# Quarter-wise first modulations in a two-layer hybrid diffusion block on one Trainium2 core

## The chip, the cores and the metric

The kernel runs on one core of one Trainium2 chip. The time is the device time of one execution in microseconds (us). Three runs of the kernel before are at hand, and one more execution was taken with the hardware profiler; every row below is from that one. Engines are named as in the profile: PE is TensorE's matmul and PEld its weight load, DVE is VectorE, ACT is ScalarE, POOL is GpSimd, SP is SyncE, which here issues the loads.

## What is computed

Two layers of a transformer-like trunk act on 512 tokens (256 latent, 256 context) of 1024 features. Each layer is a SwiGLU feed-forward half-step, three attention branches that are gated and merged, and a second feed-forward half-step. Each of these parts starts with a normalisation whose gain and shift come from a conditioning vector, the modulation:

```python
def adaln(h, g, shift, scale):
    return rms_norm(h, g) * (1 + scale) + shift

mx = jnp.split(cond_x @ ada_w[l] + ada_b[l], N_MOD, axis=-1)   # N_MOD = 9, each of 1024 features
x = x + 0.5 * mx[2] * swiglu(adaln(x, ffn1_norm[l], mx[0], mx[1]), ffn1_w_in[l], ffn1_w_out[l])
```

The context stream uses the same weights with its own conditioning vector. The change touches only the first two modulations of the first layer, `mx[0]` (shift) and `mx[1]` (scale), for both streams. They stand at the head of everything: no feed-forward product can be made before some of the normalised, modulated features are there.

## The kernel before

Activations are held transposed: features on the 128 partitions, tokens along the row. So the 1024 features are `KD` = 8 blocks `k` of 128, and a normalised activation is a pair of tiles `hh`, `hl` (a rounded part and the remainder) per block. Every weight is split in the same way into `whi` (by ACT) and `wlo` (by DVE), and one product of a 128-column weight block with a feature block is three matmuls (`mm3`, lines 101 to 103): `whi` with `hh`, `whi` with `hl`, `wlo` with `hh`, each 512 tokens wide.

`run()` opens the kernel by hand:

- `load_x` loads the eight blocks of x and sums their squares (lines 340 to 357).
- `ahead(4)` loads the first halves (feature blocks 0 to 3) of the four weight chunks that the first products use, two gate and two up chunks. Their second halves are loaded later (`second_half`, lines 166 to 168), released by a POOL copy that waits for a certain part of `ada_w`.
- `ada_first(c, slots)` works out half `c` of the two modulations. It loads eight slots of 128x1024 (feature block `k` of the conditioning vector by 512 columns of each modulation; line 288), then yields; then for each `k` it makes four matmuls of 256 columns, one on each group of 32 array columns (`ada_product`, line 280), and yields after each `k`. `set_mods` copies the sums from PSUM (DVE, line 302), yields, transposes them (PE, line 306), adds the bias (DVE, line 312) and makes the gain `G` (DVE, line 322).
- Half 0 (`first`) is worked out between the steps of the two norms. Line 1212 then multiplies x by the norm for both token halves on DVE (`vh` and `th` hold token half 0, `p` token half 1).
- `modulate(k)` makes `hh` and `hl` of block `k`, for each token half: ACT line 409 makes `hh`, POOL line 408 makes the unrounded value `w`, DVE line 410 subtracts.
- `products` makes the first 32 products (8 blocks `k`, 4 accumulators), in the order of `k`. Half 1 (`rest`) is worked out beside the first ten of them, by this list, and blocks 4 to 7 are modulated after it:

```python
at = [1, 2, 3, 4, 5, 6, 7, 8, 8, 10]
```

PE's order is the program's own. On the other engines and on the loads' queue a scheduler sets the order when the kernel is built, and each engine then works through its list in that order. The split weights live in rings of eight `whi` and eight `wlo` tiles; the eight halves of the first four chunks fill both, so the split of a later chunk needs a tile that PE has finished with.

Of the kernel before, what the change touches and what calls it, by code (L numbers as in the profile page):

```python
# [13 lines left out]
D = 1024  # L14
KD = 8
# [43 lines left out]
class Kernel:  # L59
# [221 lines left out]

    def ada_first(self, c, slots):

        acc = self.P("v", (128, 256))
        raws = []
        for k, raw in enumerate(slots):
            src = self.t["ada_w"][0, 0:2, k, :, c * 512:(c + 1) * 512]
            self.nc.sync.dma_start(out=raw.rearrange("p (m n) -> p m n", m=2), in_=src.rearrange("m p n -> p m n"))
        yield
        for k, raw in enumerate(slots):  # L290
            for g in range(4):
                self.ada_product(acc, g, self.cond[:, k], raw[:, g * 256:(g + 1) * 256], k == 0, k == KD - 1)
            yield
        yield from self.set_mods(acc, [(0, 0), (0, 1)], 4 * c, 2)

    def set_mods(self, acc, mods, k0, nj):

# [884 lines left out]
    def run(self):  # L1182
        nc = self.nc
        self.setup()
        self.done = set()
        self.load_x()
        slots = []
        for i in (6, 5, 4, 3, 1, 0):
            c = self.T(f"m{i}", [128, 2, 1024])
            slots += [c[:, j] for j in range(2)]  # L1190
        for tag in ("pth", "ptl"):
            slots += [self.T(tag, [128, 1024], bufs=2) for _ in range(2)]
        slots = slots[:KD], slots[KD:]
        self.new_h()

        self.first, self.late = True, []
        self.ahead(4)
        first = self.ada_first(0, slots[0])
        next(first)
        rest = self.ada_first(1, slots[1])  # L1200
        next(rest)
        late = [second_half(slots[1][4][0:1, 0:1]) for second_half in self.late]
        self.late = None
        norms = [self.norm(0, 0, half, False) for half in range(2)]
        xn = [self.T(tag, [128, NT], bufs=1 if tag == "th" else 3) for tag in ("vh", "vh", "vh", "th", "p", "p", "p")]
        xn = [v[:, h] for v in xn for h in HALF]
        xn = [xn[:KD], xn[KD:]]
        for half in (0, 1, 0, 1):
            next(first)
            R = next(norms[half])  # L1210
            for v, x in zip(xn[half] if R else (), self.x):
                nc.vector.tensor_tensor(out=v, in0=x[:, HALF[half]], in1=R, op=ALU.mult)
        for _ in first:
            pass

        def modulate(k):
            for half in range(2):
                self.modulate(0, 0, half, k, R, xn[half][k] if k < len(xn[half]) else None)

        def products(accs, rhs):  # L1220

            self.begin(slots[1][-1][0:1, 0:1])
            for take in late:
                take()

            at = [1, 2, 3, 4, 5, 6, 7, 8, 8, 10]
            for n in range(KD * len(accs)):
                k, (acc, wt) = n // len(accs), accs[n % len(accs)]
                self.col_product(wt, KD, rhs, acc, slice(0, NT), (k, k + 1))
                while at and at[0] == n + 1:  # L1230
                    at.pop(0)
                    next(rest)
                    if not at:
                        for kk in range(KD // 2, KD):
                            modulate(kk)
            self.setup2(slots[1][-1][0:1, 0:1])

        for k in range(KD // 2):
            modulate(k)
        self.first = products  # L1240

        pend = {
            (0, 0): [(0, m) for m in range(2, 8)],
            (0, 1): [(0, 8), (1, 0), (1, 1), (1, 2)],
            (1, 0): [(1, m) for m in range(3, 9)],
            (1, 1): [],
        }

        def ffn(l, f, halves, after):

            self.steps = self.ada(pend[l, f]) if pend[l, f] else iter(())
            gap = PACE[l, f]
            done = [0]

            def fill(blocks):
                done[0] += blocks
                while done[0] >= gap > 0:
                    done[0] -= gap
                    next(self.steps, None)

            self.ffn(l, f, halves, fill, after)
            for _ in self.steps:
                pass

        for l in range(DEPTH):
            last = l == DEPTH - 1

            def then_norm(ll, n):
                def after(half):
                    if half == 0:  # L1270
                        self.new_h()
                    ticks = [1, 3, 4, 5] if half == 0 else [3, 5, 5, 5] if n == 1 else [1, 2, 2, 2]
                    self.pending.append([0, self.norm(ll, n, half), ticks])
                return after

            ffn(l, 0, (0, 1), then_norm(l, 1))
            self.mixer(l, last, then_norm(l, 2))
            if last:
                ffn(l, 1, (0,), lambda half: None)
            else:  # L1280
                ffn(l, 1, (0, 1), then_norm(l + 1, 0))
        for k in range(KD):
            nc.sync.dma_start(out=self.out[k], in_=self.x[k][:, 0:256])
# [3 lines left out]
def _layout(inputs):  # L1287
    import numpy as np

    f = {k: np.asarray(v) for k, v in inputs.items()}  # L1290
    f32 = np.float32
    o = {}
    o["x"] = np.concatenate([f["x"][0], f["ctx"][0]], 0).T.reshape(KD, 128, NT)
    o["cond"] = np.stack([f["c"][0], f["c_ctx"]], -1).reshape(KD, 128, 2).transpose(1, 0, 2)
    o["ada_w"] = f["ada_w"][:1].reshape(1, KD, 128, 9, D).transpose(0, 3, 1, 2, 4)[:, :2]
    o["ada_t"] = f["ada_w"].reshape(DEPTH, D, 9, KD, 128).transpose(0, 2, 3, 4, 1)
    o["condb"] = np.repeat(np.stack([f["c"][0], f["c_ctx"]])[None], 128, axis=0)
    o["ada_b"] = f["ada_b"].reshape(DEPTH, 9, KD, 128).transpose(3, 0, 1, 2)
# [33 lines left out]
    for n in ("a_q_norm", "a_k_norm", "b_q_norm", "b_k_norm"):  # L1332
        g = f[n][:, p64]
        row += [g, np.roll(g, 32, axis=1)]
    for n in ("c_q_norm", "c_k_norm"):
        g = f[n][:, p96]
# [9 lines left out]
    q, k = np.arange(128)[:, None], np.arange(128)[None, :]  # L1346
    o["mask"] = np.concatenate([np.where(k <= q, 0, NEG), np.where(k >= q, 0, NEG)], 1).astype(f32)
    for n, dim in (("cs64", 64), ("cs32", 32)):
# [5 lines left out]
        c, s = np.cos(ang).astype(f32), np.sin(ang).astype(f32)  # L1354
# [27 lines left out]
```

## Time and profile before

| | us |
|---|---|
| median of 3 runs | 2152.4 (2151.74 to 2154.44) |
| profiled execution, its own time | 2153.58 |
| profiled execution, span of the records | 2151.8 |
| PE busy in the span | 2097.2 (97%) |
| DVE, ACT, POOL busy | 1526.0, 1008.5, 445.1 |

The profile's page gives busy times and shares of the whole span. The timeline lists instructions in order of time, with start, duration, engine, line, the tile written and the tiles read, and in brackets how long the engine was idle before and what released it. The chain of waits follows the end back to what released each step. The view by stretches gives each engine's busy time in a stretch and TensorE's granted clock, 1.00 for the full 2.4 GHz and 0.50 for 1.2 GHz.

### The profile page before, as it was taken

The numbers are of one execution on the slowest core, as the hardware profiler recorded it, in microseconds if no ns is written. First come the engines' busy times: TensorE is split into PE (matmuls) and PEld (weight loads), VectorE is DVE, ScalarE is ACT, GpSimd is POOL, SyncE is SP. The second block draws the span as 40 slices with busy tenths as digits, with TensorE's granted clock in tenths as the row PEclk, the third lists the DMA queues.
The fourth block names the chain that finished last, engine by engine and source line by source line (L and its number), as shares of the span: only waits on it lengthen the run. The fifth ranks groups of instructions, "written<-read, shape, count | busy, mean of one in ns | idle before, by whom it ended". The sixth has DMA issues, their size and how long they took to land.

```text
span 2151.8 us, 33450 instructions
## 1 busy us (share of the span) xinstructions
PE 2097.2 (97%) x11832; PEld 1829.3 (85%) x11832; DVE 1526.0 (71%) x3121; ACT 1008.5 (47%) x2026; POOL 445.1 (21%) x854
## 2 busy tenths in 40 slices
PE   6999999999999999999999999999999799999999
PEld 3888888888898888988888898888888798899999
DVE  5587777779888766658665666856568888986665
ACT  4323233567675664432323343232336676665554
POOL 3121110444234220202010031201105412511000
PEclk9999999999999999999999999999999899999999
DMA  8565555321113224256444326555543332345663
GB/s 297 194 203 176 175 174 167 98 79 53 45 49 104 68 64 143 79 182 199 149 153 140 107 82 204 191 173 181 175 145 110 109 99 76 104 142 177 188 187 120
DMA packets 95527, 299.17 MB, mean 139 GB/s; under 512 B 10880, under 2 KB 15616, under 8 KB 94976
## 3 DMA queue, kind: packets, MB, share of 16 engines
q1 hardware_dynamic: 95360, 297.04, 43.0%
q8 instruction: 93, 1.52, 0.3%
q14 instruction: 74, 0.61, 0.1%
HBM read 292.80 MB, written 4.19 MB: 138 GB/s over the span
## 4 chain that ended last, share of the span: by engine, by line
PE 90%; DVE 5%; ACT 1%; POOL 1%; DMA 1%; issue 1%; SPq 0%; POOLq 0%; ACTq 0%; DVEq 0%
PE pd L101 13%; PE pd L102 13%; PE pd L103 13%; PE ps L101 7%; PE ps L103 7%; PE ps L102 7%; PE pv L101 7%; PE pv L103 7%; PE pv L102 7%; PE ps L710 3%; PE pt L754 2%; PE pv L763 1%; DVE wlo L109 1%; PE pv L762 1%; POOL w L408 1%
## 5 line engine op out<-in xcount | busy, mean ns | idle before, releaser
L108 ACT ACTIVATE whi<-raw 128x512 fp32r<-128x512 f32 (+2 forms) x521 | 314.8, 611 | 466.9 <-PE pd L102 141.2
L109 DVE TENSOR_TENSOR wlo<-raw,whi 128x512 fp32r<-128x512 f32 (+2 forms) x521 | 349.9, 677 | 163.5 <-ACT whi L108 159.7
L108 ACT ACTIVATE whi<-q 128x512 fp32r<-128x512 f32 (+1 forms) x299 | 184.3, 620 | 380.2 <-PE pd L102 102.3
L101 PE MATMUL pd<-hh,whi 128*128 128x512 f32 (+1 forms) x864 | 304.5, 352 | 3.1 <-ACT hh L409 1.9
L102 PE MATMUL pd<-hl,whi 128*128 128x512 f32 (+1 forms) x864 | 302.1, 350 | 1.2 <-DVE hl L410 1.1
L103 PE MATMUL pd<-hh,wlo 128*128 128x512 f32 (+1 forms) x864 | 301.5, 349 | 0.0
L109 DVE TENSOR_TENSOR wlo<-q,whi 128x512 fp32r<-128x512 f32 (+1 forms) x299 | 200.4, 674 | 121.2 <-ACT whi L108 119.6
L154 POOL COPY q<-start 1x1 f32<-1x1 f32 x151 | 54.5, 362 | 656.2 <-DVE wlo L109 472.6
L101 PEld LDWEIGHTS pd<-hh,whi 128*128 128x128 f32 x864 | 163.8, 190 | 26.0 <-ACT hh L409 2.3
L102 PEld LDWEIGHTS pd<-hl,whi 128*128 128x128 f32 x864 | 163.9, 190 | 22.0 <-DVE hl L410 1.9
L101 PE MATMUL pv<-hh,whi 128*128 128x512 f32 (+1 forms) x512 | 182.3, 356 | 0.0
L102 PE MATMUL pv<-hl,whi 128*128 128x512 f32 (+1 forms) x512 | 182.2, 356 | 0.0
L103 PE MATMUL pv<-hh,wlo 128*128 128x512 f32 (+1 forms) x512 | 182.2, 356 | 0.0
L103 PEld LDWEIGHTS pd<-hh,wlo 128*128 128x128 f32 x864 | 163.8, 190 | 21.0
L102 PE MATMUL pd<-m,whi 128*128 128x512 f32 (+1 forms) x530 | 177.7, 335 | 0.5 <-DVE m L774 0.4
L101 PE MATMUL pd<-m,whi 128*128 128x256 f32 (+1 forms) x522 | 175.6, 336 | 0.5 <-DVE x L991 0.5
L103 PE MATMUL pd<-m,wlo 128*128 128x256 f32 (+1 forms) x522 | 174.6, 335 | 0.0
L101 PE MATMUL ps<-hh,whi 128*128 128x512 f32 (+1 forms) x480 | 169.0, 352 | 1.1 <-DVE w L495 1.1
L103 PE MATMUL ps<-hh,wlo 128*128 128x512 f32 (+1 forms) x480 | 168.1, 350 | 0.0
L102 PE MATMUL ps<-hl,whi 128*128 128x512 f32 (+1 forms) x480 | 168.1, 350 | 0.0
L736 POOL TENSOR_SCALAR p<-p,rd 128x512 f32<-128x512 f32 (+1 forms) x144 | 98.0, 685 | 295.9 <-DVE rd L734 183.0
L267 DVE SCALAR_TENSOR_TENSOR m<-pth,go,m 128x1024 f32<-128x1024 f32 x112 | 140.0, 1279 | 21.3 <-POOL go L265 12.9
(323 smaller groups left out, 4894.7 us busy)
## 6 DMA issues: line engine op xcount, KB each, us to landing
q<-ffn_in SPq DMA_DIRECT2D x86, 512.0 KB, 3.6
raw<-ffn_in SPq DMA_DIRECT2D x86, 512.0 KB, 3.9
pth<-ada_t SPq DMA_DIRECT2D x64, 512.0 KB, 4.3
ptl<-ada_t SPq DMA_DIRECT2D x64, 512.0 KB, 4.3
raw<-w_gate SPq DMA_DIRECT2D x48, 512.0 KB, 3.4
q<-ffn_out SPq DMA_DIRECT2D x32, 448.0 KB, 3.3
raw<-ffn_out SPq DMA_DIRECT2D x32, 448.0 KB, 3.3
raw<-w_br SPq DMA_DIRECT2D x41, 256.0 KB, 2.6
```

The costliest lines, as they stand in the source:

```text
L101: mm(out, lhsT=ah, rhs=bh, start=first, stop=False)
L102: mm(out, lhsT=ah, rhs=bl, start=False, stop=False)
L103: mm(out, lhsT=al, rhs=bh, start=False, stop=last)
L108: self.nc.scalar.activation(out=hi, in_=src, func=AF.Copy)
L109: self.nc.vector.tensor_tensor(out=lo, in0=src, in1=hi.bitcast(F32), op=ALU.subtract)
L154: nc.gpsimd.tensor_copy(out=raw[0:1, 0:1], in_=self.start)
L267: nc.vector.scalar_tensor_tensor(out=junk[:, i], in0=raw, scalar=go, in1=cb[:, i], op0=ALU.mult, op1=ALU.mult, accum_out=o[:, j, i:i + 1])
L408: nc.gpsimd.tensor_scalar(out=h, in0=v, scalar1=g, scalar2=s, op0=ALU.mult, op1=ALU.add)
L710: nc.tensor.matmul(s, lhsT=a, rhs=b[:, ks], start=(i == 0), stop=(i == len(ops) - 1 and not mask))
L736: nc.gpsimd.tensor_scalar(out=p[:, i], in0=p[:, i], scalar1=rd[:, i:i + 1], scalar2=1.0, op0=ALU.mult, op1=ALU.mult)
L754: nc.tensor.transpose(tr[:, kt, i * 128:(i + 1) * 128], p[qts][:, i, kt * 128:(kt + 1) * 128], self.ident)
L762: nc.tensor.matmul(o, lhsT=v, rhs=PT[0][:, kt], start=(kt == 0), stop=False)
```

## The change

The two modulations are worked out in four quarters of 256 columns each (two feature blocks) instead of two halves of 512 (four blocks). Quarter `c` has eight loads of 128x512, half the size of the loads before, from an array laid out anew so that one quarter's columns of both modulations lie together. Each group of array columns gets 128 instead of 256 columns, and `ada_first` yields after every second `k`. Quarter 0 stands where half 0 stood. Quarters 1, 2 and 3 are worked out beside products 0 to 5, 8 to 13 and 16 to 21 (counted from 0), and each is followed by the modulation of its two blocks; the next two products are those of the quarter ahead. The four second halves of weights are released by quarter 2's fifth load instead of half 1's fifth.

```diff
     def ada_first(self, c, slots):
 
-        acc = self.P("v", (128, 256))
-        raws = []
         for k, raw in enumerate(slots):
-            src = self.t["ada_w"][0, 0:2, k, :, c * 512:(c + 1) * 512]
-            self.nc.sync.dma_start(out=raw.rearrange("p (m n) -> p m n", m=2), in_=src.rearrange("m p n -> p m n"))
+            self.nc.sync.dma_start(out=raw, in_=self.t["ada_w"][c, k])
         yield
+        acc = self.P("v", (128, 128))
         for k, raw in enumerate(slots):
             for g in range(4):
-                self.ada_product(acc, g, self.cond[:, k], raw[:, g * 256:(g + 1) * 256], k == 0, k == KD - 1)
-            yield
-        yield from self.set_mods(acc, [(0, 0), (0, 1)], 4 * c, 2)
+                self.ada_product(acc, g, self.cond[:, k], raw[:, g * 128:(g + 1) * 128], k == 0, k == KD - 1)
+            if k % 2:
+                yield
+        yield from self.set_mods(acc, [(0, 0), (0, 1)], 2 * c, 1)
...
-        slots = slots[:KD], slots[KD:]
+        slots = [[v[:, c * 512:(c + 1) * 512] for v in half] for half in (slots[:KD], slots[KD:]) for c in range(2)]
...
-        first = self.ada_first(0, slots[0])
-        next(first)
-        rest = self.ada_first(1, slots[1])
-        next(rest)
-        late = [second_half(slots[1][4][0:1, 0:1]) for second_half in self.late]
+        quarters = [self.ada_first(c, s) for c, s in enumerate(slots)]
+        for quarter in quarters:
+            next(quarter)
+        first = quarters[0]
+        late = [second_half(slots[2][4][0:1, 0:1]) for second_half in self.late]
...
-            self.begin(slots[1][-1][0:1, 0:1])
+            self.begin(slots[3][-1][0:1, 0:1])
             for take in late:
                 take()
-
-            at = [1, 2, 3, 4, 5, 6, 7, 8, 8, 10]
             for n in range(KD * len(accs)):
                 k, (acc, wt) = n // len(accs), accs[n % len(accs)]
                 self.col_product(wt, KD, rhs, acc, slice(0, NT), (k, k + 1))
-                while at and at[0] == n + 1:
-                    at.pop(0)
-                    next(rest)
-                    if not at:
-                        for kk in range(KD // 2, KD):
-                            modulate(kk)
-            self.setup2(slots[1][-1][0:1, 0:1])
-
-        for k in range(KD // 2):
+
+                c, step = n // 8 + 1, n % 8
+                if c < 4 and step < 6:
+                    next(quarters[c], None)
+                    if step == 5:
+                        for kk in range(2 * c, 2 * c + 2):
+                            modulate(kk)
+            self.setup2(slots[3][-1][0:1, 0:1])
+
+        for k in range(2):
             modulate(k)
```

Three places show how the order moves. Line numbers after the change are lower by one or two.

DVE after the norms. Before, `w` (the copy of half 0's sums, line 302) stands behind all fourteen products of x with the norm, of which the last two are shown:

```order
L1212 TENSOR_TENSOR p_221<-x_5_99,pt_249 128x256
L1212 TENSOR_TENSOR p_221<-x_6_101,pt_249 128x256
L302 COPY w_294<-pv_189 128x256
L312 TENSOR_TENSOR mods_85<-pv_296,adab 128x8 x2
L322 SCALAR_TENSOR_TENSOR G_87<-mods_85,gn 128x8
```

After, quarter 0's copy stands ahead of the six for token half 1, and the bias and the gain still stand behind them:

```order
L301 COPY w_309<-pv_236 128x128
L1211 TENSOR_TENSOR p_233<-x_1_91,pt_272 128x256
L1211 TENSOR_TENSOR p_233<-x_2_93,pt_272 128x256
L1211 TENSOR_TENSOR p_234<-x_3_95,pt_272 128x256
L1211 TENSOR_TENSOR p_234<-x_4_97,pt_272 128x256
L1211 TENSOR_TENSOR p_235<-x_5_99,pt_272 128x256
L1211 TENSOR_TENSOR p_235<-x_6_101,pt_272 128x256
L311 TENSOR_TENSOR mods_85<-pv_311,adab 128x4 x2
L321 SCALAR_TENSOR_TENSOR G_87<-mods_85,gn 128x4
```

Only the copy moved ahead; what the modulation waits for kept its place behind the `p` rows.

ACT around the third part of `h`. Before, the modulation of blocks 4 to 7 (`hh`, line 409) starts straight behind the splits of the four late weight halves, and the splits of the next weight chunks (`whi_557` and on) come behind its sixth:

```order
L108 ACTIVATE whi_356<-q_46_183 128x512
L409 ACTIVATE hh_163<-vh_217,mods_85,G_87 128x256
L409 ACTIVATE hh_163<-p_221,mods_85,G_87 128x256
L409 ACTIVATE hh_163<-vh_217,mods_85,G_87 128x256
L409 ACTIVATE hh_163<-p_221,mods_85,G_87 128x256
L409 ACTIVATE hh_163<-th_218,mods_85,G_87 128x256 x2
L108 ACTIVATE whi_557<-raw_555 128x512
```

After, quarter 1's four `hh` have a late half's split (`whi_342`) among them, and the four splits of the next two chunks (`whi_651` to `whi_666`) stand ahead of quarter 2's:

```order
L408 ACTIVATE hh_163<-vh_230,mods_85,G_87 128x256
L108 ACTIVATE whi_342<-raw_165 128x512
L408 ACTIVATE hh_163<-p_234,mods_85,G_87 128x256
...
L108 ACTIVATE whi_651<-raw_649 128x512
L108 ACTIVATE whi_655<-raw_649 128x512
L108 ACTIVATE whi_662<-q_124_659 128x512
L108 ACTIVATE whi_666<-q_124_659 128x512
L408 ACTIVATE hh_163<-vh_231,mods_85,G_87 128x256
L408 ACTIVATE hh_163<-p_235,mods_85,G_87 128x256
```

The splits of later weights moved from behind the modulation to ahead of it.

POOL after the change. Behind the first four `w` (quarter 0's two blocks by two token halves; `w_328` is the last) come the copies that release the second weight halves, then the one that waits for the last of all the `ada_w` loads (`start`), and then quarter 1's:

```order
L407 TENSOR_SCALAR w_328<-p_233,G_87,mods_85 128x256
L167 COPY raw_165<-pth_159 1x1
L167 COPY q_40_171<-pth_159 1x1
L189 COPY start_340<-ptl_162 1x1
L222 COPY cs_630<-ptl_162 1x1
L154 COPY q_124_659<-start_340 1x1
L407 TENSOR_SCALAR w_416<-vh_230,G_87,mods_85 128x256
```

Quarter 1's `w` moved behind the wait for the last load; before, the same four followed the first four directly.

## Rows read from the trace of the kernel before

**Rows 1.** The profile's page, span and busiest engine

```profile
span 2151.8 us, 33450 instructions
PE 2097.2 (97%) x11832; PEld 1829.3 (85%) x11832; DVE 1526.0 (71%) x3121; ACT 1008.5 (47%) x2026; POOL 445.1 (21%) x854
```

**Rows 2.** Timeline, 20 to 30 us: start, duration, instruction, [idle before, releaser]

```profile
21.92 2.07 DVE L1212 TENSOR_TENSOR vh<-x,pt 128x256 f32<-128x256 f32 x6 [0.71 <-PE pt L383]
...
24.58 2.06 DVE L1212 TENSOR_TENSOR p<-x,pt 128x256 f32<-128x256 f32 x6
25.14 0.16 PEld L280 LDWEIGHTS pv<-m,cond 128*32 128x32 f32 x8 [0.44 <-DMA m<-ada_w]
26.57 0.41 DVE L302 COPY w<-pv 128x256 f32<-128x256 f32 x1
...
27.04 0.44 PE L306 MATMUL pv<-ident,w 128*128 128x128 f32 x2 [1.26 <-DVE w L302]
...
27.78 0.17 DVE L322 SCALAR_TENSOR_TENSOR G<-mods,gn 128x8 f32<-128x8 f32 x1
...
29.13 0.50 PE L101 MATMUL pd<-hh,whi 128*128 128x512 f32 x1 [1.66 <-ACT hh L409]
...
29.91 0.64 PE L102 MATMUL pd<-hl,whi 128*128 128x512 f32 x1 [0.28 <-DVE hl L410]
```

**Rows 3.** Chain of waits, 30 to 45 us: start, duration, what

```profile
30.98 1.01 PE pv L280 x8
...
36.49 0.57 PE pv L280 x8
37.06 0.43 PE pd L101
37.49 0.23 PE pd L102
37.72 0.24 PE pd L103
...
44.48 0.22 PE pv L306 x2
```

**Rows 4.** Timeline, 45 to 60 us, second modulation and first product of chunk five

```profile
45.01 0.17 DVE L322 SCALAR_TENSOR_TENSOR G<-mods,gn 128x8 f32<-128x8 f32 x1
...
45.72 0.59 ACT L409 ACTIVATE hh<-p,mods,G 128x256 fp32r<-128x256 f32 x1
...
46.64 0.43 DVE L410 TENSOR_TENSOR hl<-w,hh 128x256 fp32r<-128x256 f32 x1 [0.30 <-POOL w L408]
...
48.18 1.14 ACT L108 ACTIVATE whi<-raw 128x512 fp32r<-128x512 f32 x2
...
59.51 0.39 PE L101 MATMUL pv<-hh,whi 128*128 128x512 f32 x1
```

**Rows 5.** Timeline, the loads' queue (SPq) and POOL's wait for the last load

```profile
9.56 10.77 SPq L288 DMA_DIRECT2D m<-ada_w  x12
...
34.38 0.34 SPq L168 DMA_DIRECT2D raw<-ffn_in  x1
...
36.72 0.17 POOL L189 COPY start<-ptl 1x1 f32<-1x1 f32 x1 [1.76 <-DMA ptl<-ada_w]
```

**Rows 6.** By stretches: length, busy PE PEld DVE ACT POOL, granted clock, DMA share, GB/s

```profile
510.00:511.00 1.00, 0.06 (x1) 0.10 (x2) 1.00 (x4) 1.00 (x2) 0.00 (x0) 1.00 0.04 8
...
551.00:552.00 1.00, 0.09 (x1) 0.00 (x0) 1.00 (x2) 0.98 (x3) 0.69 (x2) 1.00 0.26 30
552.00:553.00 1.00, 0.86 (x5) 0.86 (x6) 0.94 (x3) 0.43 (x2) 0.00 (x0) 0.68 0.77 187
553.00:554.00 1.00, 1.00 (x5) 0.97 (x5) 0.94 (x5) 0.95 (x2) 0.44 (x1) 0.50 0.46 184
554.00:555.00 1.00, 1.00 (x5) 0.83 (x4) 0.57 (x2) 0.79 (x3) 0.25 (x1) 0.50 0.00 0
555.00:556.00 1.00, 1.00 (x8) 1.00 (x8) 0.94 (x4) 0.38 (x1) 0.00 (x0) 0.62 0.00 0
```

More of the change, by code (lines that the diff above doesn't have):

```diff
@@ L1294, in _layout @@
     o["cond"] = np.stack([f["c"][0], f["c_ctx"]], -1).reshape(KD, 128, 2).transpose(1, 0, 2)
-    o["ada_w"] = f["ada_w"][:1].reshape(1, KD, 128, 9, D).transpose(0, 3, 1, 2, 4)[:, :2]
+    o["ada_w"] = f["ada_w"][0].reshape(KD, 128, 9, 4, 256)[:, :, :2].transpose(3, 0, 1, 2, 4).reshape(4, KD, 128, 512)
     o["ada_t"] = f["ada_w"].reshape(DEPTH, D, 9, KD, 128).transpose(0, 2, 3, 4, 1)
```

## The prediction

> **What bounds the kernel now.** I read four views: the page, the timeline of the first 60 us, the chain of waits there, and the clock by stretches. The page shows PE busy for 2097.2 of 2151.8 us [rows 1]. So what the change adds to or takes from PE's work at the head should reach the end nearly whole; the order of the work behind the first 32 products is the same but for a few swapped neighbours on DVE, ACT and POOL.
>
> In the timeline the reader sees what holds PE back at the head. PE's last wait for `ada_w` ends at 25.14, after 0.44 idle. But the copy of half 0's sums starts only at 26.57, when DVE is through with the six `p` rows (24.58 + 2.06 = 26.64); the gain follows at 27.78, the first product at 29.13, its second matmul at 29.91 [rows 2]. So DVE's queue sets the start of the products, and the loads do not. Nor do they bound what follows. The last load has landed at 36.72 [rows 5], while half 1's eight steps, from 30.98 on, go at PE's own pace (36.49 is one), and the last stands two products ahead of the transposes at 44.48, near 42.3 [rows 3]. Everything from there runs on PE without a wait to 59.51, where the fifth chunk's first product starts [rows 4]. That is the mark I move.
>
> **The change, part by part.**
>
> *Start of the products.* DVE finishes the eight rows of token half 0 near 24.6, does quarter 0's copy (half as wide, at most the 0.41 of [rows 2]), then the six `p` rows (2.06), then bias and gain. The gain ended 0.47 behind the transposes (27.95 against 27.04 + 0.44); those are now done early, so it ends 0.47 behind the last `p` row, near 27.35: 0.6 earlier. This is bounded by 0, if the norm's steps, which share PE with quarter 0's eight groups of matmuls instead of four, slip as much. I take -0.4. That quarter 0's data lands some microseconds sooner than half 0's is worth nothing: the data was not last.
>
> *Steps beside products.* Half 0's eight `k` ran before the products, where PE had idle time: PE waited 1.26 and 1.66 us there [rows 2]. Now only quarter 0 does, and quarters 1 to 3 are 3 x 4 = 12 steps among the products instead of 8. One step has as many columns as one before (two `k` of 128 for one of 256). Its price: a product behind a step and the step take 0.57 + 0.43 + 0.23 + 0.24 = 1.47 us, a product alone 3 x 0.23 = 0.69 [rows 3], so 0.78 a step, and four more steps are 3.1 us. Each step now has eight matmuls instead of four and eight small weight loads; the trace has no such step, so it lies between the same time and twice 0.57, by column or by `k`. I take 0.05 more, as columns are what the row is nearest to: 12 x 0.05 = 0.6. Together +3.7. The three transposes (one each) for the pair at 0.22 [rows 3] are +0.1.
>
> *Waits at the three borders.* Before, the transposes stood behind product 9 and block 4 was due at product 16: six products of cover, and PE did not wait. Now the transposes stand behind the sixth product of each eight, and only two products (2 x 0.69) and the transpose itself (0.11) cover the way through DVE, ACT, POOL and DVE again: 1.5 us. The way itself, from the transposes at 44.48: gain until 45.18, `hh` of token half 1 until 46.31, its `hl` until 47.07 [rows 3, 4], 2.6 us. So with nothing else in the queues the second matmul of the ninth product, due at 1.5 + 0.23, waits until about 2.5 with the shorter transposes: 0.8 us. That is border 3 (block 6). At border 1 (block 2) ACT has one late half's split between the two `hh` and DVE its partner; a split is 1.14 / 2 = 0.57 [rows 4]: 1.0 us. At border 2 (block 4) four splits for the next chunks stand ahead of `hh` on ACT. Their ring tiles come free with products 12 to 15, the last only when product 15 is past its second matmul, about 1.4 after product 13. Then a split of 0.6, two `hh` (0.5 apart, 0.6 long), and `hl` behind the last split's partner on DVE: the ninth product's second matmul can start near 3.5 instead of 1.7: 1.8 us. The three together are +3.6; the bounds are 0 (if all were covered) and 3.6 plus the clock below.
>
> *Loads and POOL.* SP has 32 issues for 16. Twelve took 10.77 us, spaced by landings, and SP then idles until 34.38 [rows 5]. Twice as many of half the size keep the same bytes, and the second weight halves behind them are released sooner, not later. POOL now has its wait for the last load (36.72) ahead of quarter 1's `w`. By the steps above, product 5 ends near 38.1 and quarter 1's gain near 38.8, so the wait is over by then: 0.
>
> The sum on the profiled execution's own 2153.58: -0.4 + 3.7 + 0.1 + 3.6 = +7.0, so 2160.6. Its own time stands 1.2 above the median of the three runs; against the median it is 2152.4 + 7.0 = **2159.4**. The mark at 59.51 should move to about 66.5.
>
> **The rivals.** A measurement of this kernel can tell about 0.2%, 4.3 us, from no change.
>
> *Not slower: the borders are covered.* If at each border `hh` and `hl` come within the 1.5 us of the two products, only the steps remain: -0.4 + 3.7 + 0.1 = +3.4, 2155.8, which counts as the same. It decides at whether a gain-to-`hl` way under 1.5 us is possible. Against it: the same way took 2.6 us with no other work in between [rows 3, 4]. For it: a step may be cheaper by overlap with waits, and a stalled PE does the same work later. Chance 0.15, with smaller borders and cheaper steps counted in.
>
> *The clock falls at a border.* Near 550 PE idled, and the granted clock went from 1.00 to 0.68, 0.50, 0.50 and 0.62 in four rows of 1 us: 0.32 + 0.5 + 0.5 + 0.38 = 1.7 us lost [rows 6]. An idle stretch around 510 passed at 1.00 [rows 6]. Border 2's wait is about as long as either. One to three falls give +8.7 to +12.1, 2161.1 to 2164.5. Chance 0.2.
>
> *A step costs by `k`, not by columns.* Then each step is 0.57 longer, 12 x (0.57 - 0.05) = +6.2 more, 2165.6. For it: small matmuls with their own weight loads; against it: the two `k` have only half the columns each. Chance 0.1. The Trainium skill, "TensorE: Matmul & The Clock Gate", section "Back-to-back issue gap", speaks for something of this rival: it gives about 81 ns a matmul at 128 columns and 131 ns at 512, so a matmul gets cheaper by far less than its columns. As an estimate on a straight line between these figures, 128 columns cost 0.83 of 256, which would put a step at 0.95 us and the time at 2163.3. No run shown here has the 128-column form.
>
> *The change does not do what it says: quarter 1 waits for all loads.* If 32 smaller loads landed later, POOL's wait would hold quarter 1's `w` behind the last quarter's landing. It decides once the last load lands after about 38.8, 2.1 us later than the 36.72 of [rows 5]; 3 us later costs about 1 us, 2160.4. Chance 0.05.
>
> *Faster.* It would need the products to start several us sooner, and bias and gain stand behind the `p` rows on DVE. Chance 0.03, for a clock that by luck falls less often later on.
>
> **How the numbers follow.** The forecast has the remaining 0.47, with 2157 to 2161 as its own spread. Slower by over 0.2% is above 2156.7: 0.47 + 0.2 + 0.1 + 0.05, less 0.02 for a forecast that comes out small, is 0.80. Within 0.2%: 0.15 + 0.02 = 0.17. Faster: 0.03. The range starts at 2155.5, at the lower end of the covered borders, and ends at 2164.5 with three falls of the clock; that leaves out the step by `k` and the faster case, and part of the covered one, near 0.2.
>
> **What would show it.** The fifth chunk's first product near 66 instead of 59.51; the first product near 28.7; twelve steps of about 0.6 us between 30 and 57; PE idle 0.8 to 1.8 us ahead of the first product of blocks 2, 4 and 6, released by ACT's `hh` or DVE's `hl`, the longest at block 4 right behind four `whi` splits. Wrong would be: a first product of block 2 released by POOL straight after its copy at the last landing; no idle time at the borders; a later part of the trace that gives back or loses more than 2 us.

## The result and the profile after

| | before | after |
|---|---|---|
| median | 2152.55 (6 runs, 2151.0 to 2154.44) | 2163.89 (6 runs, 2162.41 to 2164.98) |
| profiled execution, own time | 2153.58 | 2162.99 |
| span of the records | 2151.8 | 2161.2 |

The change makes the kernel slower: ratio 1.0052, with a 95% interval of 1.0041 to 1.0062. The medians stand 11.3 us apart, the two profiled executions 9.4.

The page of the changed kernel, as [rows 1], with the group that holds the products of the head:

```profile
span 2161.2 us, 33737 instructions
...
PE 2099.2 (97%) x11960; PEld 1830.5 (85%) x11960; DVE 1527.2 (71%) x3129; ACT 1009.0 (47%) x2026; POOL 442.6 (20%) x854
...
L101 PE MATMUL pd<-hh,whi 128*128 128x512 f32 (+1 forms) x864 | 305.7, 354 | 8.3 <-ACT hh L408 6.3
```

Over the whole span PE is busy for 2.0 us more than before and idle for 7.4 more. That is a mixture: by the view by stretches, PE up to the mark of the prediction (59.51 before, 68.25 now) is busy 4.9 us more (45.48 against 40.58) and idle 3.8 more (22.77 against 18.93), and behind it busy 2.9 less and idle 3.6 more. So the head lost by longer work as well as by waits. The last row names the waits: for `hh` 6.3 us, where the same group waited 1.9 for it before.

The timeline of its start, against [rows 2]:

```profile
21.00 2.08 DVE L1211 TENSOR_TENSOR vh<-x,pt 128x256 f32<-128x256 f32 x6 [0.70 <-PE pt L382]
23.66 0.28 DVE L301 COPY w<-pv 128x128 f32<-128x128 f32 x1
23.86 2.06 DVE L1211 TENSOR_TENSOR p<-x,pt 128x256 f32<-128x256 f32 x6
...
26.10 0.16 DVE L321 SCALAR_TENSOR_TENSOR G<-mods,gn 128x4 f32<-128x4 f32 x1
...
27.44 0.79 PE L101 MATMUL pd<-hh,whi 128*128 128x512 f32 x1 [2.97 <-ACT hh L408]
...
29.36 1.08 PE L280 MATMUL pv<-m,cond 128*32 128x128 f32 x16
...
34.35 0.65 PE L280 MATMUL pv<-m,cond 128*32 128x128 f32 x16
```

The first product starts at 27.44 instead of 29.13. The first steps and products are long (1.08 and 0.79), and from 34.35 on short.

PE's waits at the three borders, and the mark, from its timeline:

```profile
39.16 0.39 PE L103 MATMUL ps<-hh,wlo 128*128 128x512 f32 x1
40.34 0.49 PE L101 MATMUL pd<-hh,whi 128*128 128x512 f32 x1 [0.79 <-ACT hh L408]
40.99 0.50 PE L102 MATMUL pd<-hl,whi 128*128 128x512 f32 x1 [0.16 <-DVE hl L409]
...
49.40 0.39 PE L103 MATMUL ps<-hh,wlo 128*128 128x512 f32 x1
51.32 0.50 PE L101 MATMUL pd<-hh,whi 128*128 128x512 f32 x1 [1.54 <-ACT hh L408]
52.67 0.50 PE L102 MATMUL pd<-hl,whi 128*128 128x512 f32 x1 [0.85 <-DVE hl L409]
...
61.06 0.40 PE L103 MATMUL ps<-hh,wlo 128*128 128x512 f32 x1
62.21 0.49 PE L101 MATMUL pd<-hh,whi 128*128 128x512 f32 x1 [0.75 <-ACT hh L408]
62.91 0.50 PE L102 MATMUL pd<-hl,whi 128*128 128x512 f32 x1 [0.20 <-DVE hl L409]
...
68.25 0.39 PE L101 MATMUL pv<-hh,whi 128*128 128x512 f32 x1
```

Six waits, 0.95 + 2.39 + 0.95 = 4.29 us idle, at the places foretold, the longest at block 4. The borders cost more than this idle time. In a stream the matmuls start 0.23 apart, so behind the `L103` shown, the last matmul ahead of the border, the second matmul of the next product, `L102`, was due 0.46 later; it started 1.37, 2.81 and 1.39 later than that. With 0.1 more until the third matmul each time, the borders took 5.9 us. The mark moved from 59.51 [rows 4] to 68.25, by 8.74.

The chain of waits behind the first border, against [rows 3]:

```profile
40.99 0.50 PE pd L102
...
41.73 0.57 PE pv L280 x16
42.30 0.43 PE pd L101
42.73 0.23 PE pd L102
42.97 0.23 PE pd L103
```

A step of two `k` in 128 columns (16 records) takes 0.57, as one `k` in 256 columns (8 records) did, and the product behind it is the same too. Behind a wait `L102` counts 0.50 in this view and not 0.23; 0.27 more at each of the six waits is the 1.6 us by which the 5.9 exceeds the idle time of 4.29.

### The profile page after: what moved, and what is told of

It is laid out like the page before. It is cut to its first block, busy times and chain, and to the rows that moved or that the text cites. A ratio compares the mean times of both kernels' runs of the same rounds, so it can differ in the third digit from the quotient of the medians.

```text
span 2161.2 us, 33737 instructions
## 1 busy us (share of the span) xinstructions
PE 2099.2 (97%) x11960; PEld 1830.5 (85%) x11960; DVE 1527.2 (71%) x3129; ACT 1009.0 (47%) x2026; POOL 442.6 (20%) x854
## 3 DMA queue, kind: packets, MB, share of 16 engines
q8 instruction: 94, 1.54, 0.3%
## 4 chain that ended last, share of the span: by engine, by line
PE 85%; DVE 7%; DMA 3%; POOL 2%; ACT 2%; issue 1%; SPq 0%; ACTq 0%; POOLq 0%; DVEq 0%
PE pd L102 12%; PE pd L101 12%; PE pd L103 12%; PE pv L103 7%; PE pv L101 7%; PE pv L102 7%; PE ps L101 7%; PE ps L103 7%; PE ps L102 7%; PE ps L709 2%; PE pt L753 2%; DVE wlo L109 2%; PE pv L762 1%; PE pv L761 1%; DMA m<-ada_w 1%
## 5 line engine op out<-in xcount | busy, mean ns | idle before, releaser
L102 PE MATMUL pd<-hl,whi 128*128 128x512 f32 (+1 forms) x864 | 302.9, 351 | 2.1 <-DVE hl L409 2.0
L103 PE MATMUL pd<-hh,wlo 128*128 128x512 f32 (+1 forms) x864 | 301.8, 349 | 0.0
L102 PEld LDWEIGHTS pd<-hl,whi 128*128 128x128 f32 x864 | 164.4, 190 | 24.0 <-DVE hl L409 4.0
L102 PE MATMUL pv<-hl,whi 128*128 128x512 f32 (+1 forms) x512 | 182.2, 356 | 0.0
L103 PE MATMUL pv<-hh,wlo 128*128 128x512 f32 (+1 forms) x512 | 182.2, 356 | 0.0
L103 PEld LDWEIGHTS pd<-hh,wlo 128*128 128x128 f32 x864 | 164.3, 190 | 20.9
L102 PE MATMUL pd<-m,whi 128*128 128x512 f32 (+1 forms) x530 | 177.0, 334 | 0.8 <-DVE m L773 0.8
L103 PE MATMUL pd<-m,wlo 128*128 128x256 f32 (+1 forms) x522 | 174.1, 333 | 0.0
L102 PE MATMUL ps<-hl,whi 128*128 128x512 f32 (+1 forms) x480 | 168.3, 351 | 0.0
L103 PE MATMUL ps<-hh,wlo 128*128 128x512 f32 (+1 forms) x480 | 168.1, 350 | 0.0
```

Of the source, the lines that this page charges most:

```text
L102: mm(out, lhsT=ah, rhs=bl, start=False, stop=False)
L103: mm(out, lhsT=al, rhs=bh, start=False, stop=last)
```

## The experiments

Each was timed beside the kernel before on one chip, and that kernel's median lay between 2151.59 and 2153.74 there, so the ratios compare better than the times; "mark" is the start of the fifth chunk's first product in its trace. Traces of one and the same head also differ in their start: the changed kernel's first product is at 27.44, and at 27.86 to 28.12 in the three runs that leave all ahead of it as it is. The edits are against the changed kernel, the last two against the kernel before. `idle(n)` makes `n` matmuls of the identity with itself, into a bank that nobody reads.

### No borders: the quarters back to back (e1_run_on)

```diff
-                c, step = n // 8 + 1, n % 8
-                if c < 4 and step < 6:
+                c, step = n // 6 + 1, n % 6
+                if c < 4:
```

> The changed kernel, but quarters 1, 2 and 3 follow one another without a pause: beside products 0 to 5, 6 to 11 and 12 to 17, so that 2, 4 and 6 products lie between a quarter's transpose and the first product of its blocks, instead of 2, 2 and 2. The fifth chunk's first product is at 68.25 us in the changed kernel and at 59.51 before. Theory (the borders wait because two products are too short a cover): the waits at the borders of blocks 4 and 6 (2.9 and 1.5 us) go, the one at block 2 (1.5 us) stays; the mark moves to about 63.9, the time falls by 4.4 us against the changed kernel and stays 7 us above the kernel before. Rival (what delays the border is the order on ACT, DVE and POOL, whatever the cover): the waits move with the blocks, the mark stays above 67.

Measured: 2156.57, ratio 1.0021 (1.0011 to 1.0031), mark 62.82. PE's timeline where block 2 starts:

```profile
38.38 0.27 PE L305 MATMUL pv<-ident,w 128*128 128x128 f32 x1
...
39.28 0.64 PE L280 MATMUL pv<-m,cond 128*32 128x128 f32 x16
...
40.75 0.65 PE L280 MATMUL pv<-m,cond 128*32 128x128 f32 x16
41.32 0.51 PE L101 MATMUL pd<-hh,whi 128*128 128x512 f32 x1
```

No wait is left at any border, at block 2 neither, where the theory kept it: there the next quarter's two steps fill the way from transposes to `hl`. The mark is 5.4 earlier than in the changed kernel, with a first product 0.5 later (27.94). So the borders cost about 5.9, as counted above, and that part of the loss is one of placing the steps, not of having quarters.

### Borders one at a time (e8_cover, e9_cover_four)

```diff
-                c, step = n // 8 + 1, n % 8
+                c, step = (n // 6 + 1, n % 6) if n < 12 else (n // 8 + 1, n % 8)
```

> The changed kernel with quarter 1 beside products 0 to 5, quarter 2 beside products 6 to 11 and quarter 3 as it was, beside products 16 to 21. Steps of a quarter now stand behind products 6 and 7, and four products instead of two stand between quarter 2's transposes and block 4. Theory (each border is a way of given length from the transposes to hl, less what PE has to do meanwhile): no wait at block 2 (-1.49 against the changed kernel's mark of 68.25); at block 4 the way was 1.5 + 2.92 = 4.4 us, four products cover 2.8, so 1.2 to 1.6 stays (-1.3 to -1.7); block 6 keeps its 1.5. Mark near 65.2, median near 2160.7. Rival (the waits are not additive: what one border gives back the next takes, because ACT, DVE or a load is late whatever PE does): mark 67 or later, with longer waits at blocks 4 or 6. Rival (block 4's wait was only the crowd on DVE and POOL, which comes at another time here): block 4 waits under 0.5, mark near 63.8.

Measured: 2163.83, ratio 1.0052 (1.0038 to 1.0066), mark 70.66. The edit did more than was meant: for products 12 and 13 the formula gives quarter 2 once more, so blocks 4 and 5 were modulated a second time. Block 4 waited 2.98 + 1.16 for that, and the run says nothing of the cover there; block 2 had no wait, as expected. The second form:

```diff
-                c, step = n // 8 + 1, n % 8
-                if c < 4 and step < 6:
+                c, step = (n // 6 + 1, n % 6) if n < 12 else (3, n - 16)
+                if 0 <= step < 6:
```

> The run with quarter 1 beside products 0 to 5, quarter 2 beside 6 to 11 and quarter 3 beside 16 to 21 once more. In the first form of it, blocks 4 and 5 were modulated twice, behind product 11 and again behind product 13, which overwrote tiles that the products of block 4 read; here each block is modulated once. Theory (each border is a way of given length, less what PE has to do meanwhile; block 2 has two steps and two products as cover, block 4 has four products): in that run quarter 2's transposes came at 45.39, the first pair of hh by 47.83 and the first hl by 47.90, and four products last until about 48.4, so no wait at block 4 and none at block 2; block 6 keeps its 1.5. Mark 68.25 - 1.49 - 2.92 = 63.8, and up to 0.7 more if the first product is as late as in that run (28.12 instead of 27.44); median about 2159.3. Rival (what the borders give back, the next one takes): a wait over 1.0 at block 4 or over 2.2 at block 6, mark 66 or later.

Measured: 2159.65, ratio 1.0029 (1.0017 to 1.0040), mark 64.35, with the first product at 27.86 (0.4 later than in the changed kernel). PE's timeline:

```profile
58.22 0.49 PE L101 MATMUL pd<-hh,whi 128*128 128x512 f32 x1 [0.76 <-ACT hh L408]
58.96 0.50 PE L102 MATMUL pd<-hl,whi 128*128 128x512 f32 x1 [0.25 <-DVE hl L409]
```

Only block 6 waits, by as much as before. The borders add up: what two of them give back is not taken by the third. Block 4's own gain has two causes that this run does not part: four products of cover instead of two, and only one split ahead of its `hh` on ACT instead of four.

### Full clock at the start (e3_after_warm, e7_run_on_after_warm)

```diff
         for _ in first:
             pass
+        self.idle(6)
```

> The changed kernel with six matmuls of no use (128 columns, float32) between quarter 0's transpose and the first product, where PE waits about 3 us. In the changed kernel the matmuls are 0.43 us apart until about 34.2 us (half clock) and 0.23 from there; in the kernel before they were 0.23 apart for a while from 23 us on and again from 33.5. Theory (part of the loss is that the first three products and two steps run at half clock): with PE kept busy these take 0.57 a step and 0.89 a product instead of 1.01 and 1.4 to 1.6, the mark moves 1 to 2.2 us earlier, to 66 to 67.2. Rival (the clock does not come up, or the added matmuls delay the first product by as much): the mark stays within 0.3 us of 68.25.

Measured: 2161.62, ratio 1.0043 (1.0028 to 1.0058). The first steps are short from the start (0.65 at 29.33 against 1.08 at 29.36), quarter 1's transposes come at 35.79 instead of 37.90, and the mark stands at 68.9 all the same, with a first product 0.45 later (27.89). What took the gain, from the timelines of POOL, ACT and PE:

```profile
36.94 0.18 POOL L189 COPY start<-ptl 1x1 f32<-1x1 f32 x1 [6.44 <-DMA ptl<-ada_w]
...
37.45 0.55 POOL L407 TENSOR_SCALAR w<-vh,G,mods 128x256 f32<-128x256 f32 x1
37.64 0.63 ACT L108 ACTIVATE whi<-raw 128x512 fp32r<-128x512 f32 x1 [0.47 <-DMA raw<-ffn_in]
38.18 0.58 ACT L408 ACTIVATE hh<-p,mods,G 128x256 fp32r<-128x256 f32 x1
38.81 0.50 PE L101 MATMUL pd<-hh,whi 128*128 128x512 f32 x1 [1.36 <-ACT hh L408]
```

Quarter 1's gain was ready at 36.53 (36.37 + 0.16). Now its `w` stands behind POOL's wait for the last `ada_w` load, and one of its `hh` behind a split whose load has just landed. In the changed kernel neither was late (POOL's `w` there waited for DVE's gain, 38.73). PE then waited 1.36 + 0.84, and the granted clock was 0.69 from 40 to 44 us.

The same six matmuls where steps cover the borders, that is in the first experiment's kernel:

> The three quarters back to back beside products 0 to 17, as in the run on those, and six 128-column matmuls of the identity with itself, into a bank nobody reads, ahead of the first product, where PE waits anyway. That run had half clock until 34.5 us, so the first products and two steps took longer. Theory (the half clock at the start costs about 1.1 to 1.5 us and is bought back by work in the gap): products and steps at full clock from the first on, mark 61.4 to 61.8 instead of 62.82, median near 2155.3. Rival (with PE earlier, the second weight halves or POOL's wait for the last load, landing near 37, become the bound): the start is 1 us earlier but PE waits at block 2 or before quarter 2's transposes for as much, mark 62.5 or later.

Measured: 2154.35, ratio 1.0007 (0.9998 to 1.0016), mark 61.89, 0.93 earlier than without them. The first product and one step are still long (0.79 at 27.97, 1.08 at 29.88), the second step short (0.64 at 32.48). So a part of the half clock was bought back, and a part stayed; the mark lies just behind the theory's range. In the first of these two runs the same matmuls at the same place gave short products from the first on (0.49 at 27.89). What decides this no run here shows.

### Quarter 1 ahead of the products (e2_quarter1_ahead, e5_quarter1_ahead_run_on)

```diff
-        late = [second_half(slots[2][4][0:1, 0:1]) for second_half in self.late]
+        late = [second_half(slots[1][4][0:1, 0:1]) for second_half in self.late]
...
+        for _ in range(5):
+            next(quarters[1])
...
+                if n == 0:
+                    next(quarters[1], None)
+                    for kk in (2, 3):
+                        modulate(kk)
...
-                if c < 4 and step < 6:
+                if 1 < c < 4 and step < 6:
```

> The changed kernel, but quarter 1's four steps run before the first product, in the time in which PE waits for quarter 0's modulation; its transpose follows product 0, and the second weight halves are released by quarter 1's fifth load instead of quarter 2's, so that POOL does not wait for them. Quarters 2 and 3 stay where they are. Theory (steps that stand among products cost 0.78 us each, and those in PE's waiting time cost nothing): 4 x 0.78 = 3.1 us go, the border of block 2 (1.5 us) goes, and up to 1 us of the half-speed start goes; the mark moves from 68.25 to between 62.6 and 63.7, the first product stays at 27.4. Rival (the steps ahead push the first product back by as much as they take, 4 x 0.57 to 4 x 1.0): only the border and the 0.2 us of switching per step are gained, the first product comes at 29 or later, the mark stays above 65.

Measured: 2160.81, ratio 1.0041 (1.0026 to 1.0056), mark 66.58. The four steps ahead cost nothing (first product at 27.63), and block 2's border is gone. That is 3.1 + 1.5 won, but only 1.7 arrive. The rest is lost at block 4; ACT's timeline, and PE's:

```profile
44.12 1.15 ACT L108 ACTIVATE whi<-raw 128x512 fp32r<-128x512 f32 x2 [4.08 <-DMA raw<-ffn_in]
45.17 1.13 ACT L108 ACTIVATE whi<-q 128x512 fp32r<-128x512 f32 x2
46.32 0.60 ACT L408 ACTIVATE hh<-vh,mods,G 128x256 fp32r<-128x256 f32 x1
...
47.46 0.80 PE L101 MATMUL pd<-hh,whi 128*128 128x512 f32 x1 [2.98 <-ACT hh L408]
```

PE came to block 4 about 5 us sooner. The four splits ahead of `hh` on ACT no longer wait for PE (47.45 in the changed kernel) but for the load of the fifth chunk, which lands at 44.1. The wait is 2.98 instead of 1.54, and the granted clock behind it was 0.64 (46 to 48 us) and 0.50 (48 to 52). Quarters 2 and 3 set back to back behind it:

```diff
-                if 1 < c < 4 and step < 6:
+                c, step = (n - 1) // 6 + 2, (n - 1) % 6
+                if n > 0 and c < 4:
```

> Both edits together: quarter 1 ahead of the products as in the second run, and quarters 2 and 3 beside products 1 to 6 and 7 to 12 without a pause. Theory (the loss is steps among products, borders without cover and a slower clock, each by itself): eight steps remain as in the kernel before, no border waits (9 and 11 products of cover), and the first product stays 1.7 us earlier than before; the mark moves from 68.25 to about 58, 1 to 2 us earlier than the 59.51 before, the time to 0.5 to 2 us below the kernel before. Rival (quarters cost something else as well, the smaller loads or the 128-column form): the mark stays 2 us or more above 59.51.

Measured: 2154.44, ratio 1.0012 (1.0003 to 1.0022), mark 61.56. That is the rival's number; what the trace shows behind it is DVE's order and a late load, not a cost of the 128-column form. DVE's and PE's timelines:

```profile
37.95 0.69 DVE L109 TENSOR_TENSOR wlo<-raw,whi 128x512 fp32r<-128x512 f32 x1 [3.93 <-ACT whi L108]
38.61 0.69 DVE L109 TENSOR_TENSOR wlo<-q,whi 128x512 fp32r<-128x512 f32 x1
39.22 0.28 DVE L301 COPY w<-pv 128x128 f32<-128x128 f32 x1
...
39.55 0.33 PE L305 MATMUL pv<-ident,w 128*128 128x128 f32 x1 [2.44 <-DVE w L301]
```

The copy of quarter 2's sums stands on DVE behind two remainders of the late weight halves. Those wait for ACT's first split, and that for its load (37.29, after 4.72 idle). Behind PE's 2.44 of waiting the granted clock was 0.83 from 40 to 42 us and 0.50 from 42 to 44, so that steps and products there were long as well. From 20 to 30 us the DMA engines are full before the change and after it (share 1.05, 387 GB/s by the view by stretches), and after it until 36 us too (1.05, 386 GB/s). POOL's copy behind the last `ada_w` load ran at 36.56 here, 37.04 in the changed kernel and 36.72 before: a head that asks for data sooner met the same landing times.

### The kernel before, with two steps in PE's waiting time (e6_before_two_ahead)

```diff
         for _ in first:
             pass
+        for _ in range(2):
+            next(rest)
...
-            at = [1, 2, 3, 4, 5, 6, 7, 8, 8, 10]
+            at = [1, 2, 3, 4, 5, 6, 6, 8]
```

> The kernel before (halves), with the first two of half 1's eight steps ahead of the first product, behind half 0's transposes, where PE waits 1.66 us; the other six beside products 0 to 5 and the transposes behind product 7. Theory (a step among products costs 0.78 us and one in PE's waiting time nothing, if its load has landed): 2 x 0.78 = 1.6 off the mark, 59.51 to 57.9, and up to 1.5 more if the clock does not fall in the gap; median 2149.5 to 2150.0. Rival (the loads bound the head: half 1's slots land near 1.4 us apart up to 36.7, so the steps ahead wait for their loads or the second half's modulation cannot start sooner): first product later than 29.6, or a new wait at block 4, mark 59 or later, median within 0.7 of the kernel before.

Measured: 2149.76, ratio 0.9986 (0.9978 to 0.9995), mark 56.20, 3.31 earlier. This is the fastest of all these kernels, ahead of both the one before and the one after, by little. PE's timeline, and the view by stretches:

```profile
27.10 1.08 PE L280 MATMUL pv<-m,cond 128*32 128x256 f32 x16
28.82 0.50 PE L101 MATMUL pd<-hh,whi 128*128 128x512 f32 x1 [0.65 <-ACT hh L409]
...
30.26 0.64 PE L280 MATMUL pv<-m,cond 128*32 128x256 f32 x8
...
30.00:32.00 2.00, 2.00 (x21) 0.80 (x19) 1.20 (x3) 1.72 (x4) 2.00 (x3) 1.00 1.05 382
```

Both terms of the theory came: 1.6 for two steps fewer among the products, and 1.4 because the clock stayed at full. The other 0.3 is an earlier first product, and the first matmul of all was 0.3 earlier already (15.44 against 15.74), which the edit does not touch. The step behind the first product takes 0.64 where it took 1.08; in the kernel before the granted clock was 0.53 from 30 to 32 us and 0.62 from 32 to 34.

### The kernel before, kept busy by idle matmuls (e4_before_warm)

```diff
+        for _ in range(5):
+            next(first)
+        self.idle(5)
         for _ in first:
             pass
+        self.idle(6)
```

> The kernel before (halves), with five 128-column matmuls of the identity ahead of half 0's transposes and six behind them, in PE's two gaps. It computes the same. Theory (the half clock from about 30 to 33 us is due to the two gaps): full clock through the head, products and steps 0.57 and 0.69 from the start, mark 1.0 to 1.7 earlier (57.8 to 58.5), median 2150.3 to 2151.0. Rival (the idle matmuls push the transposes back, or the clock falls all the same): first product later than 29.4 and mark 59.2 or later, no gain or a loss of up to 0.5.

Measured: 2152.05, ratio 0.9995 (0.9986 to 1.0004), mark 59.03. PE's timeline:

```profile
26.86 1.38 PE L398 MATMUL pd<-ident 128*128 128x128 f32 x10
28.07 0.38 PE L306 MATMUL pv<-ident,w 128*128 128x128 f32 x2
...
30.11 0.50 PE L101 MATMUL pd<-hh,whi 128*128 128x512 f32 x1 [0.32 <-ACT hh L409]
```

The steps and products are short from the first on, so in this trace filling the two gaps kept the clock. But the transposes came at 28.07 instead of 27.04, and the first product at 30.11. Some 0.6 of that is the idle matmuls ahead of the transposes, which took 1.38; 0.4 is half 0's last four steps, which took 2.91 here and 2.10 before, so that the copy of the sums started at 27.00 instead of 26.57. What the clock gave, about 1.5, was spent but for 0.5. Both sides were half right.

## Why the prediction was right, and what was mis-sized

The direction and the cause were right, and the median of 2163.89 lies in the range; the size was too small. That the range held it was in part luck: the median is above the forecast's own spread of 2157 to 2161, in the stretch that was added for falls of the clock at the borders, and the trace has no such fall. At the mark the forecast was +7.0 and the trace shows +8.74. By its steps:

- **Start of the products**: forecast -0.4, measured -1.69 (27.44 against 29.13). The reason to cut the 0.6 was that the norm might slip; it came earlier instead, 21.00 against 21.92 for the first `vh` row. The sentence that failed is that the earlier data is worth nothing: the norm's sums stand on PE behind quarter 0's first step, which waits for its first load, now half as large (first matmul at 14.65 instead of 15.74; 15.07 to 15.34 in the three runs with the same head). The other 0.8 is DVE's new order, forecast as 0.6: from the first `vh` row to the first product it is 6.44 here and in the run with one border left, and 7.21 before. As those three runs have their first product at 27.86 to 28.12, some 0.4 to 0.7 of the 1.69 is an early start of this one trace.
- **Steps**: four more at 0.78, 3.1, as forecast. The surcharge of 0.05 each was 0: 0.57 for either form. The rival by `k` is out, and with it the estimate from the Trainium skill, "TensorE: Matmul & The Clock Gate", section "Back-to-back issue gap": it gave 0.95 for a step. The 131 ns for 512 columns that it started from is not what this trace shows either, where such matmuls start 0.23 us apart.
- **Waits at the borders**: forecast 3.6, measured 5.6 counted as the forecast counts, by the delay of the second matmul, and 5.9 with the third. All three were too small: block 2 1.37 against 1.0, block 4 2.81 against 1.8, block 6 1.39 against 0.8. At block 2 the forecast's own way of 0.8 and split of 0.57 give 1.4; it took 1.0 without a reason. At block 6 it had nothing else in the queues, but token half 1 of blocks 6 and 7 has no product with the norm yet; DVE makes it there (line 405), and ACT makes both blocks' `hh` of token half 0 first, so that the `hh` needed starts 1.0 behind the first one (60.57) instead of 0.5:

```profile
61.57 1.29 ACT L408 ACTIVATE hh<-w,mods,G 128x256 fp32r<-128x256 f32 x2
61.81 0.42 DVE L405 TENSOR_TENSOR w<-x,pt 128x256 f32<-128x256 f32 x1
```

  The largest miss is block 4's way behind the `hh`:

```profile
49.05 1.24 ACT L108 ACTIVATE whi<-q 128x512 fp32r<-128x512 f32 x2 [0.26 <-PE ps L102]
49.47 0.16 DVE L321 SCALAR_TENSOR_TENSOR G<-mods,gn 128x4 f32<-128x4 f32 x1
49.71 1.29 DVE L109 TENSOR_TENSOR wlo<-q,whi 128x512 fp32r<-128x512 f32 x2
49.80 1.56 POOL L407 TENSOR_SCALAR w<-vh,G,mods 128x256 f32<-128x256 f32 x1 [5.21 <-DVE G L321]
50.19 0.58 ACT L408 ACTIVATE hh<-vh,mods,G 128x256 fp32r<-128x256 f32 x1
...
51.34 0.82 POOL L407 TENSOR_SCALAR w<-p,G,mods 128x256 f32<-128x256 f32 x1
...
52.19 0.42 DVE L409 TENSOR_TENSOR hl<-w,hh 128x256 fp32r<-128x256 f32 x1 [0.38 <-POOL w L407]
```

  ACT did what was forecast: the last ring tile comes free with a product late in the block, and `hh` starts at 50.19; the forecast's 1.4 and 0.6 behind the transposes at 48.13 give 50.1. But the way then led through POOL, which the forecast left out. The gain came late behind a remainder on DVE, and the two `w` took 1.56 + 0.82, so the second token half's `hl` ended at 52.61.
- **Half clock at the start**: not in the sum, +1.1. The same two products and two steps and a third product took 6.91 us (27.44 to 34.35) against 5.83 (29.13 to the step at 34.96): the earlier start fell wholly into the half clock. The clock column of the changed kernel shows 1.00 there while the durations are those of half clock; in the run with one border left, the same 1.08 stands at a granted clock of 0.50 (28 to 32 us). So durations are the better sign here.
- **Loads and POOL**: forecast 0, measured 0. POOL's copy ran at 37.04, quarter 1's `w` at 38.73 behind the gain. The runs with a faster PE show how near that rival was.
- **The clock at a border**: it did not fall; behind the 2.39 of waiting at block 4 the next step takes 0.64 and the matmuls 0.39 to 0.50, as at full clock. After 1.36 + 0.84 and after 2.44 of waiting in other runs it did fall (1.08 for a step at 42.87 and at 42.49). What parts these cases is not settled.

With the transposes' 0.1, -1.69 + 3.1 + 0.1 + 5.9 + 1.1 is 8.5 of the 8.74. From the mark to the end 0.7 more was lost in the profiled pair. Against the medians it is 2.6: the profiled executions lie 1.0 above their median before and 0.9 below it after. The other runs have no trace, and where their 1.9 lies stays open; so it is not shown whether the sign named for a wrong prediction, over 2 us lost in a later part, came.

## What to carry to other kernels

Cutting a piece of head work finer helps only where its pieces land in time that the bounding engine has free anyway; every piece that moves among its products is paid in full, and each hand-over through other engines needs as much work behind it as the way is long. Before cutting, look for what can be moved into a gap as it is: two steps in PE's wait gave 2.6 us together with the clock that stayed up, where four steps moved the other way and three borders cost 11.3. Price a border with the other engines' queues as they stand at that moment, and with the bounding engine's new start.

## What the runs showed of the hardware

- A step of eight 128-column matmuls on 32 array columns each takes what four of 256 columns take, 0.57 us at full clock.
- POOL's `w` of 128x256 took 0.55 alone, 0.82 beside DVE's subtraction for `hl`, and 1.56 beside two 128x512 subtractions; it ended at 51.36, DVE's two at 51.00. The Trainium skill, "SBUF — State Buffer", section "Who interferes with whom", says that a DVE instruction with two inputs in SBUF contends with a GpSimd instruction that reads SBUF, and that the order of issue decides which of the two blocks; these durations agree with that, though no run parts it from other causes.
- A wait cost PE more than its idle time. The records of a stream of 128x512 matmuls last 0.39 us and start 0.23 apart; behind a wait one lasts 0.49 or 0.50, six times. At the three borders 4.29 us idle stood for 5.9 us lost.
- In the early part of some traces the granted clock reads 1.00 while the durations are those of the lower level: steps of 1.08 at 29.36 and 31.95 in the changed kernel, where the same duration stands beside 0.50 in another run.
